# Triangular inverses of two recurrent mixers: substitution on VectorE, or doubling on TensorE

## The chip, the cores and the metric

One core of a Trainium2 chip runs the whole program in one launch. The metric is the device time of that core in microseconds (us). Engines are named as in the profile: PE (TensorE) multiplies, PEld is its weight load, DVE is VectorE, ACT is ScalarE, POOL is GpSimd, SP is SyncE, whose queue issues nearly all DMAs.

## The reference

One layer of a decoder runs over 1024 prompt tokens and 8 sequences of 4 sample tokens:

```python
h = rms_norm(x) * (1 + scale_m) + shift_m
p_a, p_b, p_c = split(h @ w_in)
y_a = rwkv7(p_a)           # mixer A: 6 heads x 64, delta rule
y_b = gated_deltanet(p_b)  # mixer B: 6 heads x 64, delta rule
y_c = hgrn2(p_c)           # mixer C: 4 heads x 64, gated, no delta rule
x = x + gate_m * (concat(y_a, y_b, y_c) @ w_out)
x = x + gate_f * ((silu(h2 @ w_gate) * (h2 @ w_up)) @ w_ffn_out)
```

The delta rule makes each token's update depend on the tokens before it. Computed by chunks of 64 tokens, a head and a chunk need the inverse of a 64x64 lower triangular matrix with ones on its diagonal (`triangular_solve` with `IA = A + eye` in the reference of mixer B; mixer A's loop over tokens is brought to the same form). With 17 chunks (16 of the prompt, one that holds the sample tokens) and 6 + 6 heads that is 204 inverses.

## The kernel before, in words

Arrays lie with channels or tokens on the 128 partitions; two heads are handled at a time, one on partitions 0 to 63 and one on 64 to 127. So mixers A and B are three pairs of heads each, C is two pairs. A pair is cut into three segments of 6, 6 and 5 chunks. A segment goes through three stages, which are the parts of `seg_a`, `seg_b`, `seg_c` between their `yield`s: stage 0 prepares whole-segment arrays, stage 1 finishes the inverses, stage 2 runs the recurrence chunk by chunk. The main loop writes stage 2 of one segment, stage 1 of the next and stage 0 of the one after beside each other, together with the projections `p` of the next pair (`dense`), which are wide PE products of 128x128 weights with 384, 288 or 296 columns, float32 as three passes over rounded halves. Behind the mixers come the output projection and the feed-forward part, in two halves of the columns (`ffn_input`, `ffn_up`, `down`), where nearly all is wide PE products with 264 columns; their weights are split into halves `wh` and `wl` by ACT, and by DVE or POOL.

The inverses, in `invert` (line 769), called by `seg_a` and `seg_b` for one segment of two heads: the four diagonal 32x32 blocks of every chunk are written to DRAM (`mb`, 4 DMAs) and read back so that each partition holds a block and every fourth column of it (`int`, 4 DMAs); a DMA sets the start of the result `ix`. DVE then substitutes through 31 columns with two instructions each (into `itq`, then into `ix`), under `nc.priority(SUBHI)`, which sets them ahead of other DVE work. The result goes back through DRAM (`tb`, 4 + 4 DMAs), DVE transposes a part (`its`), and the lower left 32x32 blocks are found by two rounds of 32x32 products on PE with ACT copies behind them.

No order is written by hand. The class `Plan` records all operations with their tiles; `Plan.order` simulates the five engines with the prices of `Plan.cost` and picks at each step the recorded operation that comes first and is ready; `emit` writes them down, and each engine then works through its list in order. Tiles of a tag are given out in the order of recording: `psm`, `psd`, `psg`, `psc` (lines 676 to 686) are two PSUM banks each, all eight there are. `mm2` (line 721) is one 64x64 product for each of the two heads, one behind the other; a float32 product is two matmuls in the trace. All operations carry line 626, that of `emit`, so rows are told apart by tiles.

Of the kernel before, what the change touches and what calls it, by code (L numbers as in the profile page):

```python
# [21 lines left out]
P = 128  # L22
# [21 lines left out]
NG = 4  # L44
FG = 2
NINT = 1
SUBHI = 3000
NITQ = 1
NITS = 2
NIX = 2  # L50
# [56 lines left out]
for _nm, _w in (("ident", 128), ("ones", 128), ("ind", 16),  # L107
                ("m3", 192), ("m3s", 192), ("neg", 64), ("negs", 64),
                ("sel1", 8), ("sel2", 8), ("reset", 448), ("bones", 128), ("bmean", 128), ("xinit", 512)):
    MASK_COLS[_nm] = (_n, _w)  # L110
    _n += _w
# [4 lines left out]
def mask_arrays():  # L116
# [31 lines left out]
    xi = np.zeros((P, 2, 8, 32))  # L148
    for v, nb in enumerate((24, 20)):
        for cg in range(NG):  # L150
            for j in range(8):
                xi[nb * cg:nb * cg + nb, v, j, NG * j + cg] = 1.0
    put("xinit", xi.reshape(P, 512))
# [26 lines left out]
class Tile:  # L180
    def __init__(self, plan, tag, dt):
        self.plan, self.tag, self.dt = plan, tag, dt
        self.slot = self.fresh = self.ap = None
        self.first = None          # first op
        self.left = 0
        self.ops = []
        self.end = 0
        self.writes, self.reads = [], []


class View:
    """a view of a tile whose place is not decided yet; kept as the view of the first place and the way to it"""
# [37 lines left out]
class Op:  # L230
    __slots__ = ("i", "eng", "fn", "args", "kw", "pre", "succ", "npre", "hold", "lat", "ready", "prio", "cols", "wait", "dense", "new", "tiles",
                 "label", "end", "start", "after", "x", "next", "load")
# [10 lines left out]
class Plan:  # L243
    """stands for nc and the tile pools while a program is written down"""
# [27 lines left out]
    def give(self, tag, to, cut):  # L272
        """once the last tile of tag is done with, the parts that cut makes of its places hold tiles of the tag to"""
# [14 lines left out]
    # ---- what a view covers  # L288
    def cover(self, v):
# [12 lines left out]
        if m is None:  # L302
            m = 1
            for s, n in dims:
# [13 lines left out]
    # ---- writing down  # L318
# [29 lines left out]
    def glue(self, ops):  # L348
        """to be issued one right after the other, once all of them can be"""
# [14 lines left out]
    def dep(self, o, p, kind):  # L364
        # kind 2: result needed, 1: only the order matters
# [32 lines left out]
    # ---- prices  # L398
    def cost(self, o):
# [7 lines left out]
        e = o.eng  # L407
        if e == "tensor":
# [11 lines left out]
            # hold: how long the next one has to wait; load: how long after the one before the weights are there  # L420
# [45 lines left out]
    # ---- the order  # L466
    def order(self):
# [12 lines left out]
        # queue of the tiles of each tag  # L480
# [16 lines left out]
        bw = [0.0]  # L497
        warm = {}
# [34 lines left out]
        while len(seq) < n:  # L533
# [109 lines left out]
class Step:  # L643
# [7 lines left out]
    # tiles of one tag are given out in program order, so every stream of work has its own  # L651
# [27 lines left out]
    def psm(self):  # L679
        return self.nc.tile("ps", [P, 512], F32, "psm", 2)  # L680
# [8 lines left out]
    def load_consts(self, par, masks, lora):  # L689
# [6 lines left out]
        self.masks = masks  # L696
# [28 lines left out]
    def tokens(self, arrs, c, nch):  # L725
        """chunk c of each array [(h, d), tokens] -> psum [64 tokens, array, h, d]; two chunks are turned at once"""
# [8 lines left out]
    def headsum(self, x, n, which="bones", alloc=None):  # L735
        """sum or mean over the channels of a head, on each of its channels; the ones are exact in float32r"""
# [8 lines left out]
    def sigmoid(self, out, x, nbias=0.0, sign=1.0):  # L745
        """sigmoid(sign * x - nbias) from the one table set that has exp and ln"""
# [12 lines left out]
    def table(self, name, behind=None, before=None):  # L759
        """load a set of functions, behind one activation and before another"""  # L760
# [7 lines left out]
    # tt[(h,s), c, t] holds N^T, N = -(strictly lower part); on return it holds ((I - N)^-1)^T  # L768
    def invert(self, tt, nc_):
        nc = self.nc  # L770
        nb = 4 * nc_
        mb = self.nc.tile("dr", [2, 2, nc_, 32, 32], F32, f"mb{nc_}", 3)
        for h in (0, 1):
            for b in (0, 1):
                o = CH * h + 32 * b
                nc.sync.dma_start(mb[h, b].rearrange("c s t -> s c t"), tt[o:o + 32, :, 32 * b:32 * b + 32])
        nt = self.nc.tile("sb", [P, 32, 32], F32, "int", NINT)
        mf = mb.rearrange("h b c s t -> (h b c) s t")
        for cg in range(NG):
            nc.sync.dma_start(nt[nb * cg:nb * cg + nb], mf)  # L780
        # one 32x32 block and every fourth column of it per partition:
# [1393 lines left out]
```

## Time and profile before

| | us |
|---|---|
| median of 3 runs | 1865.06 |
| lowest and highest of them | 1862.27, 1881.21 |
| profiled execution, first to last instruction | 1864.7 |
| PE busy in it | 1715.9 (92%) |
| DVE busy | 1557.1 (84%) |
| ACT busy | 952.0 (51%) |
| POOL busy | 958.8 (51%) |

The profile gives no other time of its execution than that span. A busy share is a mean over stages with different limits; up to about 100 us the inputs come in, from there to about 920 us the mixers run, behind them the output projection, and from 1065 us on the feed-forward part. Matmul ends are modelled, so PE counts as busy for longer than a matmul keeps the next one waiting.

### The profile page before, as it was taken

The page shows a single profiled execution, that of the slowest core. Times are in us where ns is not written, and L with a number is a line of the kernel's source. Part 1 is how long each engine was busy: PE and PEld are TensorE (multiplying, and loading weights), DVE is VectorE, ACT ScalarE, POOL GpSimd, SP SyncE. Part 2 cuts the span into 40 slices and gives each one's busy share as a digit, 9 for nine tenths or more (in the row PEclk, how much of TensorE's full clock was granted, in tenths as well). Part 3 has the DMA queues.
Part 4 walks back from the last instruction along what each step waited for, and adds up shares of the span by engine and source line. Part 5 has one row for each costly group of instructions (what it writes and reads, how often), then busy time and mean ns, then how long its engine had stood idle before and what let it go on. Part 6 is the DMA issues. An engine that isn't in the chain of part 4 may idle for free.

```text
span 1864.7 us, 42417 instructions
## 1 busy us (share of the span) xinstructions
PE 1715.9 (92%) x15462; PEld 1483.8 (80%) x15462; DVE 1557.1 (84%) x3981; ACT 952.0 (51%) x2383; POOL 958.8 (51%) x1089
## 2 busy tenths in 40 slices
PE   4999999899899789899999999999998889999996
PEld 2777766667677677677679999999998789999995
DVE  6776688879879877887776999889999999899998
ACT  4543454655556455656874655444444543443444
POOL 5542333433335544636523866656567555555555
PEclk8989999889999898999989999999999799999998
DMA  7424123123224222211353222323232132232231
GB/s 264 124 64 116 39 62 109 49 68 113 59 77 127 55 63 55 57 34 39 102 155 115 66 93 95 108 91 109 91 103 69 62 115 79 91 108 85 87 108 65
DMA packets 151242, 166.56 MB, mean 89 GB/s; under 512 B 65941, under 2 KB 91161, under 8 KB 151033
## 3 DMA queue, kind: packets, MB, share of 16 engines
q1 hardware_dynamic: 150456, 163.27, 28.8%
q8 instruction: 121, 1.98, 0.5%
q14 instruction: 89, 0.72, 0.1%
q10 hardware_dynamic: 576, 0.59, 0.1%
HBM read 149.23 MB, written 14.57 MB: 88 GB/s over the span
## 4 chain that ended last, share of the span: by engine, by line
PE 52%; DVE 28%; issue 6%; POOL 5%; ACT 4%; SPq 2%; DMA 2%; DVEq 0%; POOLq 0%; ACTq 0%
PE psd L626 16%; PE psc L626 13%; PE psm L626 11%; PE psg L626 11%; DVE sl L626 6%; DVE itq L626 5%; DVE ix L626 5%; DVE kp L626 3%; SPq L626 2%; POOL wl L626 2%; DVE s L626 2%; ACT sl L626 2%; DVE wl L626 2%; DVE wr L626 2%; DVE act L626 1%
## 5 line engine op out<-in xcount | busy, mean ns | idle before, releaser
L626 PE MATMUL psd<-act,wh 128*128 128x384 f32 (+3 forms) x2144 | 552.8, 334 | 13.2 <-ACT act L626 7.4
L626 PEld LDWEIGHTS psd<-act,wh 128*128 128x128 f32 x2144 | 373.9, 195 | 40.8 <-ACT act L626 8.9
L626 POOL TENSOR_TENSOR wl<-wr,wh 128x512 fp32r<-128x512 f32 (+1 forms) x216 | 300.7, 1396 | 192.1 <-ACT wh L626 177.3
L626 PE MATMUL psd<-act,wl 128*128 128x384 f32 (+3 forms) x1048 | 348.9, 333 | 5.3 <-DVE wl L626 3.8
L626 ACT ACTIVATE sl<-sl 128x384 f32<-128x384 f32 (+5 forms) x400 | 188.1, 484 | 129.2 <-DVE sl L626 101.4
L626 ACT CAST wh<-wr 128x512 fp32r<-128x512 f32 (+1 forms) x280 | 170.7, 615 | 109.0 <-PE psd L626 27.8
L626 PEld LDWEIGHTS psd<-act,wl 128*128 128x128 f32 x1048 | 203.7, 194 | 21.2 <-DVE wl L626 6.2
L626 DVE TENSOR_TENSOR itq<-int,ix 96x66 f32<-96x66 f32 (+26 forms) x558 | 170.7, 306 | 27.1 <-DMA int<-mb 15.9
L626 DVE TENSOR_TENSOR ix<-ix,itq 96x66 f32<-96x66 f32 (+26 forms) x558 | 164.7, 295 | 9.6
L626 PE MATMUL psg<-act,wh 128*128 128x264 f32 (+2 forms) x784 | 154.2, 290 | 5.3 <-DVE act L626 4.0
L626 PE MATMUL psc<-act,wh 128*128 128x264 f32 (+2 forms) x776 | 152.4, 289 | 0.8 <-DVE act L626 0.6
L626 PE MATMUL psm<-act,wh 128*128 128x264 f32 (+1 forms) x760 | 147.8, 288 | 2.7 <-ACT act L626 1.3
L626 POOL TENSOR_TENSOR sl<-sl,sl 128x384 fp32r<-128x384 f32 (+5 forms) x84 | 85.5, 1019 | 101.2 <-ACT sl L626 39.2
L626 PEld LDWEIGHTS psg<-act,wh 128*128 128x128 f32 x784 | 124.6, 191 | 7.5 <-DVE act L626 4.9
L626 ACT CAST raw<-sl 128x264 fp32r<-128x264 f32 x88 | 36.3, 413 | 173.7 <-DVE sl L626 92.5
L626 PEld LDWEIGHTS psc<-act,wh 128*128 128x128 f32 x776 | 123.1, 190 | 2.4 <-DVE act L626 1.1
L626 PEld LDWEIGHTS psm<-act,wh 128*128 128x128 f32 x760 | 119.5, 190 | 4.5 <-ACT act L626 1.5
L626 POOL TENSOR_TENSOR wl<-int,wh 128x512 fp32r<-128x512 f32 (+1 forms) x63 | 87.9, 1398 | 61.1 <-ACT wh L626 61.0
L626 PE MATMUL psc<-act,wl 128*128 128x264 f32 (+2 forms) x388 | 113.4, 292 | 5.4 <-DVE wl L626 3.7
L626 PE MATMUL psg<-act,wl 128*128 128x264 f32 (+2 forms) x392 | 114.0, 291 | 2.6 <-DVE wl L626 2.1
L626 PE MATMUL psm<-act,wl 128*128 128x264 f32 (+1 forms) x380 | 110.2, 290 | 4.4 <-DVE wl L626 3.0
L626 ACT COPY ts<-psg 64x128 f32<-64x128 f32 (+1 forms) x272 | 75.9, 279 | 69.1 <-PE psc L626 46.1
(324 smaller groups left out, 4481.3 us busy)
## 6 DMA issues: line engine op xcount, KB each, us to landing
wr<-in_w_fi_dram SPq DMA_DIRECT2D x87, 256.0 KB
wr<-in_w_ada_dram SPq DMA_DIRECT2D x80, 256.0 KB
wr<-in_w_in_dram SPq DMA_DIRECT2D x62, 256.0 KB
wr<-in_w_fo_dram SPq DMA_DIRECT2D x51, 256.0 KB
int<-in_w_fi_dram SPq DMA_DIRECT2D x46, 256.0 KB
kp<-in_xT_dram SPq DMA_DIRECT2D x32, 192.0 KB
tq<-in_w_fi_dram SPq DMA_DIRECT2D x23, 256.0 KB
s<-in_w_fi_dram SPq DMA_DIRECT2D x20, 256.0 KB
```

The source lines that it names most:

```text
L626: getattr(getattr(nc, o.eng), o.fn)(*[real(a) for a in o.args], **{k: real(a) for k, a in o.kw.items()})
```

## The change

`invert` is written anew. It starts from the identity and doubles the size of the inverted diagonal blocks: for blocks of 1 it copies the places one below the diagonal; for blocks of 2, 4, 8, 16 and 32 it forms `T N T` on PE, with a DVE transpose in front and an ACT copy between, and writes the places that the level's mask names (`lvm`, in use by mixer C before) with `copy_predicated` on DVE. It is recorded as a whole in stage 1. `N` is masked as it leaves PSUM. The DRAM round trips, `itq`, `its` and the initial values are gone; `int` has two tiles (`NINT`), `ix` one. Of the two `psm` banks one becomes `psi`, which the inverses use for both products of a level; mixer C takes `psi` and `psm` in turn, and the feed-forward part goes through banks in a cycle of eight.

The planner's prices change too: a wide matmul holds PE for its columns plus 12 ns (3 before), each 64x64 product 58 ns (110 and 27 before), and operations of POOL that read SBUF and operations of DVE that read two SBUF operands (or one, for copies and `tensor_scalar`) get a `port`, which only one of them at a time can hold in the simulated order. Comments and docstrings are removed as well; the other constants that set engines in the feed-forward part stay.

```diff
-NINT = 1
-SUBHI = 3000
+NINT = 2
+NIX = 1
...
+        o.port = e == "gpsimd" and len(sb) > 0 or e == "vector" and (
+            len(sb) > 1 or len(sb) == 1 and o.fn in ("tensor_scalar", "tensor_copy"))
...
-                o.hold = max(M, n) / 2.4 + 3 if n >= 256 else max(M / 1.2, n / .6)
+                o.hold = max(M, n) / 2.4 + 12 if n >= 256 else max(M / 1.2, n / .6)
...
-                o.hold = 27 if p0 >= 64 else 2 * max(M, n) / 1.2 + 3
+                o.hold = 2 * max(M, n) / 2.4 + 5
...
+            if o.port:
+                tm = max(tm, port)
+                port = tm + o.hold
...
     def psm(self):
-        return self.nc.tile("ps", [P, 512], F32, "psm", 2)
+        return self.nc.tile("ps", [P, 512], F32, "psm", 1)
+
+    def psi(self):
+        return self.nc.tile("ps", [P, 512], F32, "psi", 1)
...
+    def inverse_tiles(self, n):
+        x = fl(self.nc.tile("sb", [P, 6, P], F32, "int", NINT))
+        return x[:, 0:n], x[:, 384:384 + n]
+
+    def invert(self, tt, nt, t, nch):
+        nc = self.nc
+        n = nch * CH
+        c3 = lambda a: a.rearrange("p (c t) -> p c t", t=CH)
+        fill = lambda li, x: nc.vector.copy_predicated(
+            c3(tt), self.lvm[:, 0, li].unsqueeze(1).broadcast_to([P, nch, CH]), c3(x))
+        nc.scalar.copy(c3(tt), self.lvm[:, 0, 6].unsqueeze(1).broadcast_to([P, nch, CH]))
+        fill(0, nt)
+        for li in range(1, 6):
+            nc.vector.transpose(t, tt)
+            px = self.psi()
+            for c in range(nch):
+                sl = slice(c * CH, (c + 1) * CH)
+                self.mm2(px[:, sl], nt[:, sl], t[:, sl], True, True)
+            x = self.nc.tile("sb", [P, 384], F32, "ix", NIX)[:, 0:n]
+            nc.scalar.copy(x, px[:, 0:n])
+            py = self.psi()
+            for c in range(nch):
+                sl = slice(c * CH, (c + 1) * CH)
+                self.mm2(py[:, sl], x[:, sl], tt[:, sl], True, True)
+            fill(li, py[:, 0:n])
...
-        nc.vector.tensor_copy(tt, pm[:, 0:n])
+        nt, ti = self.inverse_tiles(n)
+        cp = nch - (si == 2)
+        nc.vector.tensor_tensor(t3(nt)[:, 0:cp], t3(pm[:, 0:n])[:, 0:cp],
+                                self.m("m3")[:, 0:CH].unsqueeze(1).broadcast_to([P, cp, CH]), op=ALU.mult)
...
-        next(inv, None)
+        self.invert(tt, nt, ti, nch)
...
-            pa = self.psm()
+            pa = (self.psm, self.psi)[li % 2]()
...
-        return (self.psd, self.psg, self.psc, self.psm)[self.turn % 4]()
+        return (self.psd, self.psg, self.psc, self.psm, self.psd, self.psg, self.psc, self.psi)[self.turn % 8]()
```

DVE's list in the middle of the mixers, before: the substitution of one segment stands between the other work of two stages.

```order
L626 TENSOR_TENSOR ix_169<-ix_169,itq_170 96x5x12
L626 TENSOR_TENSOR gs_180<-psg_152,msk_63 128x192
L626 TENSOR_TENSOR itq_170<-int_113,ix_169 96x6x11
L626 SCALAR_TENSOR_TENSOR sl_312_11426<-raw_229_8027,par_90,sl_312_11426 128x256
L626 TENSOR_TENSOR ix_169<-ix_169,itq_170 96x6x11
L626 TENSOR_TENSOR kp_79<-psm_111,sl_298_10956 128x384
L626 TENSOR_TENSOR itq_170<-int_113,ix_169 96x6x10
L626 SCALAR_TENSOR_TENSOR sl_291_10835<-sl_291_10835,sl_308_11124 128x384
L626 TENSOR_TENSOR ix_169<-ix_169,itq_170 96x6x10
L626 TENSOR_TENSOR kp_65<-sl_291_10835,gb_154 128x384
```

DVE's list now, at an inverse of a mixer A segment (`kp_69` is its `tt`, `S` the recurrence's state, `sd` the decayed one):

```order
L624 TENSOR_SCALAR sd_180<-S_168,dl_163 128x64
L624 COPY_PREDICATED kp_69<-lvm_93,psi_165 128x320
L624 SCALAR_TENSOR_TENSOR sl_191_7110<-sl_189_7054,par_90,raw_139_4654 128x384
L624 STREAM_TRANSPOSE int_113<-kp_69 128x320
L624 TENSOR_REDUCE mod_89<-psm_111 128x9 x2
L624 TENSOR_SCALAR mod_89<-mod_89,par_90 128x9 x2
L624 SCALAR_TENSOR_TENSOR S_167<-psc_117,dl_163,sd_180 128x64
L624 TENSOR_SCALAR sd_181<-S_167,dl_163 128x64
L624 COPY_PREDICATED kp_69<-lvm_93,psi_165 128x320
L624 STREAM_TRANSPOSE int_113<-kp_69 128x320
L624 SCALAR_TENSOR_TENSOR S_169<-psc_118,dl_163,sd_181 128x64
```

The 62 instructions of a substitution have given way to six predicated copies and five transposes, and other segments' work stands between them.

PE's list before, around the products of one inverse (`psd<-act,wh` and `psd<-act,wl` are projections):

```order
L626 MATMUL psc_118<-its_174,kp_73 32x32
L626 MATMUL psd_151<-act_123,wh_101 128x296
L626 MATMUL psd_151<-act_124,wh_101 128x296
L626 MATMUL psm_111<-msk_63,sl_114_2960 128x128 x2
L626 MATMUL psc_118<-its_174,kp_73 32x32 x11
L626 MATMUL psd_151<-act_123,wl_105 128x296
L626 MATMUL psd_151<-act_125,wh_101 128x296
L626 MATMUL psd_151<-act_126,wh_101 128x296
L626 MATMUL psd_151<-act_125,wl_105 128x296
L626 MATMUL psd_151<-act_127,wh_103 128x296
L626 MATMUL psc_117<-kp_73,its_174 32x32
L626 MATMUL psd_151<-act_128,wh_103 128x296
```

PE's list now, around one level of an inverse:

```order
L624 MATMUL psd_151<-act_121,wh_101 128x384
L624 MATMUL psi_165<-int_112 64x64 x12
L624 MATMUL psd_151<-act_122,wh_101 128x384
L624 MATMUL psd_151<-act_121,wl_105 128x384
L624 MATMUL psd_151<-act_123,wh_101 128x384
L624 MATMUL psd_151<-act_124,wh_101 128x384
L624 MATMUL psm_111<-wr_96,ct_88 32x256 x2
L624 MATMUL psm_111<-wr_98,ct_88 32x256 x2
L624 MATMUL psd_151<-act_123,wl_105 128x384
L624 MATMUL psi_165<-kp_66,ix_166 64x64 x12
L624 MATMUL psd_151<-act_125,wh_101 128x384
```

In place of two rounds of 32x32 products in a segment there are ten sets of 64x64 products, each for six chunks of two heads, with projections and other narrow work between them.

## Rows read from the trace of the kernel before

**Rows 1.** The page: its first line.
```profile
span 1864.7 us, 42417 instructions
```

**Rows 2.** Busy time by stretch: us, each engine's us (instructions), PEclk granted, DMA share.
```profile
100.00:860.00 760.00, 695.07 (x7152) 531.04 (x7153) 608.79 (x1942) 403.72 (x1150) 319.37 (x504) 0.94 0.26 71
860.00:920.00 60.00, 58.98 (x738) 43.38 (x736) 38.89 (x93) 46.54 (x140) 35.64 (x60) 1.00 0.22 67
920.00:1065.00 145.00, 141.09 (x1265) 125.68 (x1265) 107.82 (x235) 83.79 (x226) 72.99 (x89) 0.95 0.40 120
1065.00:1400.00 335.00, 331.42 (x2680) 327.49 (x2679) 304.89 (x593) 162.23 (x334) 204.46 (x148) 1.00 0.30 96
1520.00:1850.00 330.00, 314.69 (x2509) 307.70 (x2508) 303.93 (x723) 142.57 (x284) 189.51 (x139) 1.00 0.27 87
```

**Rows 3.** Chain of waits, 600 to 700 us: share of the stretch by line.
```profile
by line: PE psd L626 16.3%; DVE ix L626 14.4%; DVE itq L626 12.8%; DVE sl L626 8.2%; SPq L626 7.7%; PE psc L626 7.5%; DMA int<-mb 5.6%; issue 4.4%; POOL sl L626 2.9%; ACT sl L626 2.5%; POOL wl L626 2.1%; POOL sd L626 2.0%; PE psm L626 2.0%;
```

**Rows 4.** Timeline of DVE: start us, us, engine, line, operation, out<-in.
```profile
604.93 0.93 DVE L626 TENSOR_TENSOR itq<-int,ix 80x42 f32<-80x42 f32 x1
605.89 0.93 DVE L626 TENSOR_TENSOR ix<-ix,itq 80x42 f32<-80x42 f32 x1
...
611.47 0.18 DVE L626 TENSOR_TENSOR ix<-ix,itq 80x24 f32<-80x24 f32 x1
```

**Rows 5.** Timeline of POOL at the same time.
```profile
605.76 1.00 POOL L626 TENSOR_TENSOR kp<-sl,sl 128x384 f32<-128x384 f32 x1
```

**Rows 6.** Timeline of PE, with the idle time before in brackets.
```profile
612.13 0.34 PE L626 MATMUL psd<-act,wh 128*128 128x384 f32 x1
615.22 1.01 PE L626 MATMUL psm<-sl,kp 64*64 64x64 f32 x14 [2.74 <-DVE sl L626]
```

**Rows 7.** Busy time just behind that wait.
```profile
615.00:618.00 3.00, 2.79 (x28) 2.67 (x29) 2.58 (x4) 0.33 (x1) 2.63 (x6) 0.50 0.35 83
```

**Rows 8.** Groups by line: xcount | busy us, mean ns | idle before.
```profile
L626 DVE TENSOR_TENSOR itq<-int,ix 96x66 f32<-96x66 f32 (+26 forms) x558 | 170.7, 306 | 27.1 <-DMA int<-mb 15.9 <-DMA kp<-tb 1.8
...
L626 DVE TENSOR_TENSOR ix<-ix,itq 96x66 f32<-96x66 f32 (+26 forms) x558 | 164.7, 295 | 9.6
...
L626 DVE STREAM_TRANSPOSE its<-kp 32x192 f32<-32x192 f32 (+1 forms) x36 | 12.7, 354 | 3.6 <-DMA kp<-tb 3.0
...
L626 DVE COPY_PREDICATED kp<-lvm,psm 128x384 f32<-128x384 uint8 (+5 forms) x48 | 23.4, 499 | 7.8 <-PE psm L626 7.6
...
L626 ACT COPY raw<-psd 128x384 f32<-128x384 f32 (+4 forms) x110 | 40.5, 389 | 36.6 <-PE psd L626 35.6
...
L626 PEld LDWEIGHTS psc<-kp,its 32*32 32x32 f32 x408 | 10.6, 111 | 6.6 <-issue 2.1 <-ACT sl L626 1.8 <-ACT its L626 1.0
```

**Rows 9.** Timeline of PE: a set of 24 narrow matmuls between wide ones.
```profile
683.63 0.34 PE L626 MATMUL psd<-act,wl 128*128 128x384 f32 x1
683.80 0.33 PE L626 MATMUL psd<-act,wh 128*128 128x384 f32 x1
684.06 0.91 PE L626 MATMUL psm<-sl,kp 64*64 64x64 f32 x24
684.91 0.45 PE L626 MATMUL psd<-act,wh 128*128 128x384 f32 x1
```

**Rows 10.** Timeline of PE: narrow pairs one behind the other.
```profile
563.29 0.28 PE L626 MATMUL psc<-kp,S 64*64 64x64 f32 x4
563.40 0.28 PE L626 MATMUL psm<-sl,kp 64*64 64x64 f32 x4
```

**Rows 11.** Chain of waits over the span: start us, us, what.
```profile
1191.26 1.79 DVE wr L626
...
1223.83 1.80 DVE int L626
...
1592.48 1.76 DVE wr L626
...
1626.90 1.76 DVE s L626
```

More of the change, by code (lines that the diff above doesn't have):

```diff
@@ L147, in mask_arrays @@
     put("reset", np.broadcast_to(r, (P, 448)))
[L148 to L153, printed above, removed]
     lv = np.zeros((P, 2, 7, CH), np.float32)
@@ L231 @@
     __slots__ = ("i", "eng", "fn", "args", "kw", "pre", "succ", "npre", "hold", "lat", "ready", "prio", "cols", "wait", "dense", "new", "tiles",
-                 "label", "end", "start", "after", "x", "next", "load")
+                 "label", "end", "start", "after", "x", "next", "load", "port")
 class Engine:
@@ L407, in cost @@
         e = o.eng
+        sb = [a for a in list(o.args[1:]) + list(o.kw.values()) if isinstance(a, View) and self.space[a.t.tag] == "sb" and size(a) > 1]
+        o.port = e == "gpsimd" and len(sb) > 0 or e == "vector" and (
+            len(sb) > 1 or len(sb) == 1 and o.fn in ("tensor_scalar", "tensor_copy"))
         if e == "tensor":
@@ L497, in order @@
         bw = [0.0]
+        port = 0
         warm = {}
@@ L765, in table @@
             self.nc.after(p, before)
-    def invert(self, tt, nc_):
+    def inverse_tiles(self, n):
+        x = fl(self.nc.tile("sb", [P, 6, P], F32, "int", NINT))
+        return x[:, 0:n], x[:, 384:384 + n]
+    def invert(self, tt, nt, t, nch):
         nc = self.nc
[L771 to L780, printed above, removed]
-        x = self.nc.tile("sb", [P, 8, 32], F32, "ix", NIX)
-        tq = self.nc.tile("sb", [P, 8, 32], F32, "itq", NITQ)
-        np_ = nb * NG
-        o = MASK_COLS["xinit"][0] + (0 if nc_ == 6 else 256)
-        nc.sync.dma_start(fl(x)[0:np_], self.masks[0:np_, o:o + 256])
-        with nc.priority(SUBHI):
-            for j in range(31):
-                ni = 31 - j
-                m = j // NG + 1
-                nv = nt[0:np_, j:j + 1, j + 1:32].broadcast_to([np_, m, ni])
-                xv = x[0:np_, 0:m, j:j + 1].broadcast_to([np_, m, ni])
-                nc.vector.tensor_tensor(tq[0:np_, 0:m, 0:ni], nv, xv, op=ALU.mult)
-                nc.vector.tensor_tensor(x[0:np_, 0:m, j + 1:32], x[0:np_, 0:m, j + 1:32], tq[0:np_, 0:m, 0:ni], op=ALU.add)
-        tb = self.nc.tile("dr", [nb, 8, NG, 32], F32, f"tb{nc_}", 3)
-        for cg in range(NG):
-            nc.sync.dma_start(tb[:, :, cg], x[nb * cg:nb * cg + nb])
-        tv = tb.rearrange("(h b c) m g i -> h b c (m g) i", h=2, b=2)
-        ts = self.nc.tile("sb", [P, 6, 32], F32, "its", NITS)
-        for h in (0, 1):
-            o = CH * h
-            for b in (0, 1):
-                nc.sync.dma_start(tt[o + 32 * b:o + 32 * b + 32, :, 32 * b:32 * b + 32],
-                                  tv[h, b].rearrange("c j i -> j c i"))
-            nc.vector.transpose(ts[o:o + 32, 0:nc_], tt[o:o + 32, :, 0:32])
-            nc.gpsimd.memset(tt[o + 32:o + 64, :, 0:32], 0.0)
-        yield
-        pa = self.psc()
-        pb = self.psc()
-        for c in range(nc_):
-            for h in (0, 1):
-                o = CH * h
-                nc.tensor.matmul(pa[o + 32:o + 64, 32 * c:32 * c + 32],
-                                 tt[o:o + 32, c, 32:64], ts[o:o + 32, c, :], start=True, stop=True)
-        for h in (0, 1):
-            o = CH * h
-            nc.scalar.copy(fl(ts[o + 32:o + 64, 0:nc_]), pa[o + 32:o + 64, 0:32 * nc_])
-        for c in range(nc_):
-            for h in (0, 1):
-                o = CH * h
-                nc.tensor.matmul(pb[o:o + 32, 32 * c:32 * c + 32],
-                                 ts[o + 32:o + 64, c, :], tt[o + 32:o + 64, c, 32:64], start=True, stop=True)
-        for h in (0, 1):
-            o = CH * h
-            nc.scalar.copy(tt[o:o + 32, :, 32:64], pb[o:o + 32, 0:32 * nc_].rearrange("p (c t) -> p c t", t=32))
@@ L1250, in seg_b @@
         yield
-        next(inv, None)
+        self.invert(tt, nt, ti, nch)
         nc.gpsimd.tensor_tensor(ttv, ttv, bt[:, c0:c1].unsqueeze(2).broadcast_to([P, nch, CH]), op=ALU.mult)
@@ L1549, in ada @@
         if early == "int":
-            e = fl(nc.tile("sb", [P, 32, 32], F32, "int", NINT))
+            e = [fl(nc.tile("sb", [P, 6, P], F32, "int", NINT))[:, 0:512] for i in (0, 1)]
         for qt in range(4):
@@ L1557, in ada @@
             else:
-                xv = e[:, 256 * (qt - 1):256 * (qt - 1) + 512] if early == "int" and qt % 2 else fl(self.wr())
+                xv = e[qt // 2] if early == "int" and qt % 2 else fl(self.wr())
                 xv = xv.rearrange("p (k n) -> p k n", n=256)
@@ L2051 @@
         nc.give(tag, "wr", lambda ap: [fl(ap)[:, o:o + KH * P].rearrange("p (k n) -> p k n", n=P)
-                                       for o in range(0, ap.shape[1] * ap.shape[2], KH * P)])
+                                       for o in range(0, ap.shape[1] * ap.shape[2] - KH * P + 1, KH * P)])
     nc.order()
```

16 lines of the change are left out of this document (4 added, 12 removed).

## The prediction

> **What bounds the kernel now.** I start from the busy time by stretch [rows 2]. Behind 1065 us PE is full: its weight load is busy 327 of 335 us, 98%, at a granted clock of 1.00. In the mixers, from 100 to 860 us, PE counts as busy for 695 of 760 us, but matmul ends are modelled; the weight load, which must run once for every matmul, is busy for 531 us, 70%. So the array is not full where the change works. It could hold more matmuls, and something else decides when they come.
>
> What that is, the chain of waits tells [rows 3]: from 600 to 700 us a quarter of it is the substitution (`ix` and `itq` 27%) and another 13% is SP's queue and the landing of `int`, most of which is the same inverse's way through DRAM. The groups by line give its size [rows 8]: 558 + 558 instructions, 170.7 + 164.7 = 335 us of DVE's 609 in this stretch.
>
> The reader should then see why these are so dear. Free of POOL such an instruction takes 0.18 us; while POOL adds and multiplies, it takes 0.93 us and ends when POOL's does [rows 4, 5]: 604.79 + 1.00 and 605.76 + 1.00 on POOL, 604.93 + 0.93 and 605.89 + 0.93 on DVE. At 0.20 us each 1116 instructions would take 223 us, so about 112 of the 335 us are waits behind POOL. Since the substitution has priority in the planned order, other DVE work comes late, and PE's list stands still: it waits 2.74 us for `sl` [rows 6], and just behind that wait the granted clock is 0.50, the 1.2 GHz level [rows 7]. Over 760 us the mean is 0.94 [rows 2], so 12% of the time, 91 us, went at the lower level, where wide products take twice as long: 46 us are lost to that.
>
> **The change part by part.** Removed from DVE: 335 us and 12.7 us of small transposes [rows 8]. Added per inverse of a segment, 18 times: six predicated copies and five transposes. The copies cost 0.50 us each [rows 8], 108 of them 54 us. A transpose of 128x384 is not in the trace: the nearest row has 32x192 at 0.354 us [rows 8], so it lies between that and twice as much, 0.71; I take 0.52, close to the copy of as many columns, 90 of them 47 us (32 to 64). DVE's 609 us become about 609 - 348 + 101 = 362, 48% of the stretch. The masking of `N` takes the place of a copy of the same size. ACT gains 108 copies of 0.389 us [rows 8], 42 us on 404 of 760: hidden by its idle time; without that they would lengthen each level by 0.4 us. It loses 72 small copies, for which I count nothing. SP loses 17 DMAs per inverse, 306 in all, counted in the code, and POOL two small memsets per inverse.
>
> PE gains 10 products per chunk and pair of heads: 102 chunks make 1020 `mm2`, 4080 matmuls. Pairs one behind the other start 0.11 to 0.12 us apart [rows 10], 117 us in all. A set of six pairs alone between wide products takes 684.06 to 684.91, 0.85 us [rows 9]; 170 such sets make 145 us. I take 125, nearer the first, for a reason that follows. The 32x32 products leave: two groups of 10.6 us of weight load [rows 8], of which one is shown. Net +104 us, bounds +96 and +124.
>
> So the load that PE has to carry in this stretch goes from 531 to 635 us. At today's 70% fill the stretch would take 907 us, 147 more; at the feed-forward part's 98% it would take 648, 112 less. **Break-even is a fill of 635/760 = 84%.** Which fill comes? For a low one speaks the stretch from 860 to 920 us, where no substitution runs and the load share is 43/60 = 72% [rows 2]; but there ACT is at 78%, and the planned order leaves only 163 of the 2208 wide projection products behind the last inverse to fill gaps with. In the new order 480 stand there. For a high one speaks the next stretch, 920 to 1065 us: 126/145 = 87%, with DVE at 74% and a mix of waits. I take that, 87%: 635/0.87 = 730, **-30 us**. DVE falls to half its load, the priority that made the rest late is gone, and half of the time at the lower clock should go with the waits before it; this lies within the 87%. For the range I keep 79% (804, +44) and 95% (668, -92).
>
> The switch between wide and narrow products has a price of its own: wide ones follow each other by 0.17 us, the first narrow one comes 0.26 us behind a wide one, and a set is 0.85 where six pairs make 0.69 [rows 9, 10]. That is 0.25 us for each stretch of narrow work among wide. The Trainium skill, "TensorEngine Tiling (Array Packing)", section Key Properties, says that a change of tiling mode drains the engine, which speaks against 180 new sets; by that rule, with every set a stretch of its own, the price is 180 x 0.25 = 45 us, and the sum below would be +2 instead of -43. The trace agrees on the drain. But counted over PE's whole list between the first and the last projection, stretches of narrow work go from 520 to 460: most sets stand beside other narrow rows. So I add nothing for it.
>
> An inverse's time: before, 62 instructions at 0.3 us [rows 8] are 19 us, and three ways through the queue besides. Now five levels, each a transpose (0.52), two sets (0.85 or less), an ACT copy (0.39) and a predicated copy (0.50), with some 0.25 us of handing over at each of five places (an estimate from the 0.26 us behind a wide matmul): 4.4 us, 22 us for an inverse. Eighteen of them, all through the one `psi` bank, make 390 of 760 us: the bank can hold that, and what is late next is the chain of chunks behind it, not the bank.
>
> The stretch of mixer C gains a little from the 317 products more that are left to fill it: 60 us x (87 - 72)% = 9 us at most, nothing at least; I take -4.
>
> In the feed-forward part only the planned order moves (port, 12 ns, cycle of banks). Its first half repeats every 32.57 us (1191.26 to 1223.83), its second at 34.42 (1592.48 to 1626.90) [rows 11] with a load share of 98% and 93% [rows 2]. The work per period is the same on PE; DVE has 16 small additions more. If the new order mended all of it, 330/34.42 = 9.6 periods x 1.85 = 18 us would go. DVE is busy for 304 of 330 us there [rows 2], part of it behind POOL, and only that part can be mended, so I take half, **-9**, bounds -18 and +9 (an order that avoids overlaps in the plan and brings weights later).
>
> Sum: -30 - 4 - 9 = -43 on the span of 1864.7 us [rows 1]. The median of the runs is 1865.06, 0.4 above it, so the forecast is 1822 us.
>
> **The rivals.**
> No change: PE fills to 81 to 84%. The stretch then takes 756 to 784 us, and with -13 elsewhere the time is 1848 to 1876, middle 1862. For it: PE counted as busy 91% already, and 104 us come on top. Against it: the 70%.
>
> Slower, by the single banks. Before, `psm` had two: while one was read, the next product went into the other. Now about 137 products of the mixers (5 per segment of A, 4 of B, 4 of C, 2 for each of 16 modulation jobs) take turns in one, and 180 sets in `psi`. After each PE must find other work for as long as the reader takes, 0.50 us [rows 8], and a handover of 0.25: 317 x 0.75 = 238 us, and tiles are given out in the order of recording, so that a late one holds up all behind it. It decides as soon as more than 30/238 = 13% of that is exposed; with a third, 79 us, the time is 1822 + 79 = 1901. For it: the 72% between 860 and 920, and 2208 products that must be spread over all gaps. Against it: DVE, the reader of many, has half its load. The Trainium skill, "Perfetto Trace Analysis", section Matmuls, asks to rotate independent groups through different banks so that reading one overlaps the next group; by that rule alone two serial products on one bank are the wrong choice. No run so far shows one bank.
>
> The change doesn't do what it says: the planned port is no lock on the chip, so DVE and POOL meet as before. Then the feed-forward part gives 0 instead of -9, 1831. I give that 4 in 10 within each case; it moves none to another side by itself.
>
> **How the numbers follow.** Runs of this kernel can be told apart at about 1%: 1846 and 1884. Forecast 0.57 (its own range 1765 to 1846), no change 0.20, slower 0.23. The range reaches from a 95% fill, 1864.7 - 92 - 9 = 1764, to the slower rival, 1905; faster 0.57, same 0.20, slower 0.23.
>
> **What would show it.** Right: no `itq`; DVE near half of the mixer stretch; sets of 24 matmuls on `psi` within 0.9 us; the weight load at 84% or more there and granted clock above 0.95; no PE wait for `sl` above 2 us; the second feed-forward half below 34 us a period. Wrong: PE waiting for ACT or DVE in front of `psm` and `psi` products for more than 30 us in sum, a load share that stays near 75%, or a transpose above 0.71 us.

## Result and the profile after

The changed kernel takes **1873.57 us** (median of 20 runs, 1870.91 to 1876.53). Beside it the kernel before took 1857.26 (20 runs, 1851.52 to 1881.21): the ratio is **1.0081, 95% interval 1.0071 to 1.0092**, slower by 16 us. The forecast was 1822. The profiled run of before (1865.06) lies 7.8 us above its median, so the two traces differ by 5.9 us of span only. Its granted clock over the span was 0.953; runs of before that took about 1858 us had 0.956 to 0.959, so I put these 7.8 us down to more time at the low clock than usual, as an estimate. The traces still show where 43 us of forecast gain went.

First line of the page, answering to [rows 1], and the busy time by stretch, in the columns of [rows 2]:

```profile
span 1870.6 us, 47447 instructions
```

```profile
100.00:860.00 760.00, 756.33 (x10649) 598.93 (x10647) 462.81 (x1033) 436.64 (x1244) 301.30 (x480) 1.00 0.19 57
860.00:920.00 60.00, 60.00 (x494) 53.09 (x493) 30.73 (x55) 36.37 (x88) 26.51 (x36) 1.00 0.26 77
920.00:1065.00 145.00, 135.94 (x1351) 125.04 (x1350) 106.29 (x241) 85.49 (x227) 74.31 (x99) 0.98 0.34 103
1065.00:1400.00 335.00, 330.57 (x2638) 323.83 (x2638) 302.41 (x585) 157.97 (x324) 207.14 (x148) 1.00 0.31 96
1520.00:1850.00 330.00, 319.28 (x2508) 310.50 (x2507) 295.52 (x713) 142.71 (x283) 189.66 (x138) 0.99 0.29 87
```

In the mixers every sign of a stalled PE is gone: busy 756 of 760 us (695 before), granted clock 1.00 (0.94). DVE fell from 609 to 463 us. And yet the weight load is busy for 79% only. The mixers' last narrow product starts at 974.0 us before and at 974.6 after, so one window holds the mixers of both; first before, then after:

```profile
100.00:974.00 874.00, 806.00 (x8440) 612.59 (x8440) 688.61 (x2129) 488.10 (x1408) 372.95 (x592) 0.94 0.27 75
```

```profile
100.00:974.00 874.00, 862.45 (x11767) 688.69 (x11765) 537.23 (x1193) 513.02 (x1453) 351.84 (x558) 1.00 0.21 62
```

The same stretch of time holds 3327 more matmuls; DVE's 151 us less are worth nothing. The chain of waits from 600 to 700 us answers to [rows 3]: it is PE from end to end.

```profile
by line: PE psd L624 48.4%; PE psi L624 24.6%; PE psc L624 12.8%; PE psm L624 8.7%; PE psg L624 5.8%
```

What waits is now the other side. All waits of PE from 100 to 935 us, and two rows of all engines' waits (us in total, times, longest):

```profile
PE psm L624 <- DVE kp L624: 1.7, 3, 0.7
PE psd L624 <- ACT sl L624: 1.6, 1, 1.6
PE psi L624 <- DVE kp L624: 1.5, 1, 1.5
PE psm L624 <- ACT sl L624: 1.2, 1, 1.2
PE psm L624 <- DMA wr<-in_w_ada_dram: 0.3, 1, 0.3
PE psm L624 <- ACT tk L624: 0.2, 1, 0.2
...
DVE kp L624 <- PE psi L624: 55.7, 49, 3.2
ACT ix L624 <- PE psi L624: 53.7, 43, 4.9
```

PE waits 6.5 us in all; the inverses wait for PE. Groups by line from 100 to 935 us, answering to [rows 8]:

```profile
L624 PE MATMUL psi<-int 64*64 64x64 f32 x2040 | 88.1, 222 | 0.0
L624 PE MATMUL psi<-kp,ix 64*64 64x64 f32 x2040 | 84.2, 222 | 0.0
...
L624 DVE COPY_PREDICATED kp<-lvm,psi 128x384 f32<-128x384 uint8 (+2 forms) x103 | 57.7, 561 | 65.7 <-PE psi L624 55.7 <-ACT sl L624 4.4 <-ACT us L624 1.6
L624 DVE STREAM_TRANSPOSE int<-kp 128x384 f32<-128x384 f32 (+1 forms) x90 | 49.2, 548 | 0.6
```

The parts cost what was forecast: 4080 matmuls, transposes 49 us (47 forecast), predicated copies 0.56 us (0.50). So do the sets, in PE's timeline:

```profile
640.46 0.68 PE L624 MATMUL psm<-sl,kp 64*64 64x64 f32 x16
640.98 0.87 PE L624 MATMUL psi<-int 64*64 64x64 f32 x24
641.68 0.40 PE L624 MATMUL psm<-sl,kp 64*64 64x64 f32 x8
...
642.64 0.33 PE L624 MATMUL psd<-act,wh 128*128 128x384 f32 x1
642.90 0.92 PE L624 MATMUL psi<-kp,ix 64*64 64x64 f32 x24
643.75 0.44 PE L624 MATMUL psd<-act,wh 128*128 128x384 f32 x1
```

A set among narrow products takes 0.70 us (640.98 to 641.68). Between wide ones it takes 0.85, and the wide one ahead of it holds PE for 0.26 instead of 0.17.

**PE's time taken apart.** For every trace I split the time between 100 us and the mixers' last narrow product, from each matmul's start to the next one's. *Work* is what the shape takes among its equals (0.17 us for 128x384, 29 ns for a 64x64 record, 10.5 for one of 32x32 in quarters, 16 in the kernel before). The excess over it is a *change of shape* if the next matmul has another array shape (at most 0.2 us each), a *wait* above 0.2 us, *low clock* where the granted clock is 0.50, and *rest*. Pauses and changes of shape in a stretch at the low clock stand in that column alone, and the numbers in brackets leave those changes out (with them there are 1048 before and 1039 in the changed kernel). From 100 to 974 us of the changed kernel the profile has PE idle for 11.6 us (874.00 - 862.45); in the rest of the 21 us of waits PE counts as busy, since ends are modelled. In us:

| kernel | runs (median) | mixers end | work | changes (number) | waits | low clock | rest |
|---|---|---|---|---|---|---|---|
| before | 1857 | 974.0 | 570 | 122 (959) | 77 | 63 | 42 |
| changed | 1874 | 974.6 | 682 | 126 (1035) | 21 | 4 | 41 |
| sets_twice | 1995 | 1091.1 | 803 | 121 (1006) | 22 | 4 | 42 |
| turn_twice | 1886 | 985.9 | 683 | 128 (1058) | 25 | 7 | 44 |
| inv32 | 1861 | 960.6 | 640 | 152 (1262) | 23 | 10 | 35 |
| mixed6 | 1885 | 975.7 | 639 | 123 (988) | 48 | 22 | 43 |
| mixed6_lock | 1882 | 982.1 | 643 | 104 (875) | 54 | 37 | 44 |
| mixed6_lock_runs10 | 1879 | 985.2 | 647 | 75 (646) | 68 | 58 | 37 |
| before_newplan | 1942 | 1048.8 | 575 | 96 (785) | 106 | 133 | 39 |
| after_noport | 1912 | 1002.2 | 679 | 128 (1042) | 37 | 14 | 44 |
| after_oldplan | 1952 | 1060.0 | 679 | 141 (1117) | 53 | 38 | 49 |
| two_banks | 1965 | 1059.6 | 679 | 123 (1022) | 55 | 54 | 50 |
| setglue | 1860 | 965.6 | 685 | 114 (959) | 17 | 11 | 40 |
| runs6 | 1835 | 937.8 | 685 | 93 (833) | 16 | 5 | 39 |
| long_runs | 1849 | 949.9 | 684 | 76 (660) | 43 | 14 | 33 |
| glue_runs10 | 1859 | 961.7 | 685 | 76 (660) | 31 | 37 | 32 |
| glue_runs16 | 1899 | 997.7 | 688 | 74 (602) | 74 | 29 | 33 |
| blocks_runs16 | 1911 | 1017.3 | 646 | 96 (775) | 78 | 73 | 26 |
| before_runs6 | 1887 | 995.1 | 567 | 85 (704) | 109 | 94 | 41 |
| blocks_runs6 | 1818 | 919.0 | 641 | 117 (1054) | 14 | 13 | 35 |

The first two lines are the result: 112 us of work came, 56 us of waits and 59 us of low clock went, and the 122 us of changes stayed.

### The profile page after: what moved, and what is told of

Read it like the earlier page. It is cut to its first block, busy times and chain, and to the rows that moved or that the text cites. A ratio compares the mean times of both kernels' runs of the same rounds, so it can differ in the third digit from the quotient of the medians.

```text
span 1870.6 us, 47447 instructions
## 1 busy us (share of the span) xinstructions
PE 1782.7 (95%) x18726; PEld 1562.3 (84%) x18726; DVE 1385.9 (74%) x3030; ACT 979.4 (52%) x2423; POOL 935.4 (50%) x1050
## 4 chain that ended last, share of the span: by engine, by line
PE 80%; DVE 10%; ACT 4%; issue 2%; DMA 2%; POOL 1%; SPq 0%; DVEq 0%; ACTq 0%; POOLq 0%
PE psd L624 29%; PE psc L624 15%; PE psg L624 13%; PE psi L624 12%; PE psm L624 10%; DVE sl L624 3%; DVE kp L624 3%; DVE wl L624 1%; ACT wh L624 1%; ACT sl L624 1%; DVE act L624 1%; DMA wr<-in_w_ada_dram 1%; DVE raw L624 1%; ACT L624 1%; DVE s L624 1%
## 5 line engine op out<-in xcount | busy, mean ns | idle before, releaser
L624 POOL TENSOR_TENSOR wl<-wr,wh 128x512 fp32r<-128x512 f32 (+1 forms) x203 | 283.8, 1403 | 242.5 <-ACT wh L624 227.1
L624 ACT ACTIVATE sl<-sl 128x384 f32<-128x384 f32 (+4 forms) x400 | 186.9, 483 | 52.7 <-DVE sl L624 45.3
L624 POOL TENSOR_TENSOR wl<-int,wh 128x512 fp32r<-128x512 f32 (+1 forms) x75 | 104.9, 1401 | 92.9 <-ACT wh L624 85.1
L624 POOL TENSOR_TENSOR sl<-sl,sl 128x384 fp32r<-128x384 f32 (+6 forms) x84 | 83.7, 996 | 127.9 <-DVE sl L624 65.4
L624 ACT CAST wh<-int 128x512 fp32r<-128x512 f32 x112 | 68.6, 616 | 80.5 <-PE psg L624 26.7
L624 DVE COPY_PREDICATED kp<-lvm,psi 128x384 f32<-128x384 uint8 (+2 forms) x110 | 61.0, 555 | 65.7 <-PE psi L624 55.7
L624 DVE TENSOR_TENSOR sl<-sl,sl 128x264 f32<-128x264 f32 (+2 forms) x136 | 97.0, 721 | 13.4 <-ACT sl L624 12.4
L624 PE MATMUL psi<-int 64*64 64x64 f32 x2040 | 88.1, 222 | 0.0
L624 PEld LDWEIGHTS psi<-int 64*64 64x64 f32 x2040 | 71.6, 134 | 19.8 <-issue 10.8
L624 PEld LDWEIGHTS psi<-kp,ix 64*64 64x64 f32 x2040 | 69.7, 135 | 18.4 <-issue 9.2
```

The source lines that it names most:

```text
L624: getattr(getattr(nc, o.eng), o.fn)(*[real(a) for a in o.args], **{k: real(a) for k, a in o.kw.items()})
```

## Experiments

Theory A: PE is full, a microsecond of its work or of its changes of shape is a microsecond of the end. Rivals: the chain of one inverse through its single bank (B), or something else while PE has room (C). A ratio is to the kernel before, timed beside each run, with its 95% interval. The median of the kernel before was 1857 to 1860 us in every set of runs, so differences to the changed kernel's 1873.57 hold to about 3 us.

### More work on PE, more work on DVE

```diff
+                for _ in (0, 1):                     # sets_twice, for px and for py
                     self.mm2(px[:, sl], nt[:, sl], t[:, sl], True, True)
...
             nc.vector.transpose(t, tt)
+            nc.vector.transpose(t, tt)               # turn_twice
```

> The changed kernel with each product of the inverses issued twice into the same place: 170 sets of 24 matmul records more on PE, each 0.70 us long by the changed kernel's timeline (640.98 to 641.68), and nothing more for any other engine. Theory A (PE is full in the mixers: waits below 7 us there, granted clock 1.00): the whole 170 x 0.70 = 119 us come out at the end, 1985 to 2000. Theory B (the chain of one inverse through the single psi bank decides): 10 sets x 0.70 = 7 us more on an inverse of some 40 us, with other work beside it; 18 in a row give up to 126, so that A and B agree here unless PE has room, and the run with doubled transposes tells them apart. Theory C (PE still has room, something else decides): below 40 us.

> The changed kernel with each of the 90 transposes of the inverses done twice on DVE: 0.55 us more at each level of an inverse and 49 us more DVE work, nothing more on PE. Theory A (PE is full): within 10 us of the changed kernel's 1873.6, since DVE is at 61% in the mixers. Theory B (the chain of the inverses decides): 18 inverses in a row, each 2.7 us longer, give 49 us, 1915 to 1925.

`sets_twice` took 1994.9 us, 121 more than the changed kernel, as A has it to 2 us. `turn_twice` took 1886.1, 12.5 more: 2.5 over A's bound (4 us of waits, 3 of low clock and 2 of changes of shape more), far from B's 49. The chain through `psi` is not the limit; PE is.

### Less work on PE: 32x32 blocks

```diff
-                self.mm2(px[:, sl], nt[:, sl], t[:, sl], True, True)
+                self.mm4([(px[o:o + 32, 32 * c:32 * c + 32], v[o:o + 32, c, o % CH:o % CH + 32],
+                           tv[o:o + 32, c, o % CH:o % CH + 32]) for o in (0, 32, 64, 96)])
```

> The changed kernel with the same ten products per inverse cut to 32x32 blocks: for the first four levels the four diagonal blocks of a chunk as four matmuls on four quarters of the array, for the last one the 32x32 corner product. Transposes, predicated copies and their number stay. A set of 24 records of 32x32 took 0.40 us in the kernel before, one of 64x64 0.70. If four of them run side by side, 170 sets get 0.30 us shorter: theory A gives 51 us less than 1873.6, about 1822, and the weight-load share says nothing of it. If they go two by two, a set of the first levels takes 0.8 us and theory A gives 1870 to 1885. Theory C (something other than PE decides): 1870 to 1876 whatever a set takes.

1860.5 us (ratio 1.0016, 0.9998 to 1.0035), 13 less than the changed kernel; none of the three expectations. PE's timeline of this kernel shows a set of 48 records, 0.55 us to the next start; the four quarters run side by side in part.

```profile
639.74 0.34 PE L624 MATMUL psd<-act,wh 128*128 128x384 f32 x1
640.01 0.62 PE L624 MATMUL psi<-kp,ix 32*32 32x32 f32 x48
640.56 0.33 PE L624 MATMUL psc<-sd,ts 64*64 64x64 f32 x4
```

Work fell by 42 us, and a third shape brought 227 changes more, 26 us. The difference, 16, is near the 13 seen. That made the changes of shape the next question.

### Fewer changes of shape

One number of the planner: once a wide product is taken, at least so many follow where there are any. `setglue` binds the twelve products of a set in the order; `glue_runs16` and `glue_runs10` do both; the blocks are `inv32`.

```diff
-        run, RUN = 0, int(self.params.get("run", 0))
+        run, RUN = 0, int(self.params.get("run", 6))      # runs6; 10 in long_runs; 16
...
-                self.mm2(px[:, sl], nt[:, sl], t[:, sl], True, True)
+            self.mset([(px[:, sl], nt[:, sl], t[:, sl]) for sl in cs])   # setglue: one glued list
```

> The changed kernel with one number of the planner set: once a wide product is chosen, at least ten wide ones follow where there are any. The work is the same; the planned PE list changes between wide and narrow shapes 689 times instead of 1046. In the changed kernel's trace a narrow product that is followed by a wide one, and a wide one followed by a narrow one, each start the next about 0.1 us later than between equals (642.64 to 642.90 and 642.90 to 643.75 beside 0.17 and 0.70). Theory A (PE is full, and the changes of shape are part of what fills it): 357 x 0.1 = 36 us less than 1873.6, 1830 to 1845. The theory of the prediction (the changes of shape can be left out of the sum): within 8 us of 1873.6. A rival: narrow work comes later, the chain of chunks decides instead, 1880 or more, with waits before psc and psm products.

> The changed kernel with the twelve matmuls of a set bound together in the planned order. In the changed kernel's trace the 180 sets lie in 278 pieces; the planned list has 970 changes of shape instead of 1046. Theory A: 76 x 0.1 = 8 us less than 1873.6, 1860 to 1870. If changes of shape cost nothing: within 4 us.

> The changed kernel with the sets bound together and at least sixteen wide products in a row: 642 changes of shape in the planned list, against 1046 of the changed kernel (1873.6), 689 with runs of ten (1848.7) and 970 with bound sets (1859.9). Theory A: 404 x 0.1 = 40 us less at most, 1833 to 1846. If runs that long make the chain of chunks late: waits before psc, psi or psg products above 40 us and 1850 or more.

> The same with the products cut to 32x32 blocks, whose sets took 0.55 us from start to the next product instead of 0.70 to 0.85 but brought a third shape (1278 changes; now 883, 163 fewer than the changed kernel). Theory A: 42 us less for the products and 17 us less for the changes, 1873.6 - 59 = 1815 at best, 1815 to 1840. If the third shape eats it: like the run without blocks, 1833 to 1846.

> The changed kernel with runs of at least six wide products where there are any: 859 changes of shape in the planned list, against 1046 (1873.6) and 689 with runs of ten (1848.7). If changes of shape are the floor: 187 x 0.1 = 19 us less, 1852 to 1860, between the two. If the gain of the runs of ten came from another order by chance: anything outside 1848 to 1874.

> The changed kernel with bound sets and runs of ten: 722 changes of shape. If the loss of the run with sixteen came from the length of the runs: like long_runs, 1840 to 1855. If it came from binding the sets beside long runs (a bound set can start only when all its operands are there, and a run holds it off): 1865 to 1900 with more than 50 us of waits.

`long_runs` 1848.7 (ratio 0.9939, 0.9918 to 0.9960) and `setglue` 1859.9 (1.0009, 0.9995 to 1.0023): 25 and 14 us less than the changed kernel; A's numbers were 4 us lower for the one and just above for the other. `glue_runs16` 1898.9 (1.0210) and `blocks_runs16` 1911.2 (1.0275) went the other way, to none of A's ranges: few changes (602 and 775), but waits of 74 and 78 us and more low clock. `runs6` gave **1834.8 (0.9873, 0.9843 to 0.9902)**, better than I expected (1852 to 1860): 33 us less in changes, 5 less in waits, and the mixers end 37 us sooner. It lies in the range (outside 1848 to 1874) that I had set aside for a gain by another order by chance. Against chance speaks that the changes saved account for 33 of the 37 us; the other lengths, below, show that the order counts as well. Against the changed kernel's row above, its weight load in the same window rose from 689 to 719 us, but that window now holds 36 us of the output projection too:

```profile
100.00:974.00 874.00, 865.08 (x12076) 719.32 (x12075) 548.03 (x1231) 525.34 (x1476) 366.48 (x570) 1.00 0.23 68
```

`glue_runs10` came to 1858.6 (0.9999): as many changes as `long_runs`, and between my two cases. So runs of ten and more are paid twice: PE waits longer (31 to 78 us against 16 with six), as if narrow work that others wait for came late, and more of its time is at the low clock (14 to 73 us against 5). Six is the best length tried; the lengths between were not.

### Part of the work back on DVE

The middle segment of every mixer A and B (six of eighteen inverses) goes by substitution again.

```diff
+ROWS = lambda m, g, si: si == 1
...
-        self.invert(tt, nt, ti, nch)
+        if ROWS("a", g, si):
+            next(inv, None)                 # the substitution of the kernel before
+        else:
+            self.invert(tt, nt, ti, nch)
```

> The changed kernel with the middle segment of each mixer A and B (36 of 102 chunks, 6 of 18 inverses) solved by substitution on DVE again, as in the kernel before, and the planner without the lock for the port (with it the substitution cost the kernel before 84 us). Theory A (PE is full in the mixers, DVE has room at 61%): 36/102 x 119 = 42 us less PE work and some 110 us more on DVE, 1825 to 1845. The rival: six substitutions bring back the waits and the lower clock of the kernel before, in which case 1850 to 1875.

> Six of eighteen inverses by substitution on DVE, and the planner with the lock as in the changed kernel; 920 changes of shape in the planned list. Theory A (PE full, a microsecond of work is worth a microsecond): 43 us less work (639.4 against 682.5 in the mixers of the run without the lock) and 126 x 0.1 = 13 us less for changes of shape, 1820 to 1850. The rival: under the lock each of 372 substitution instructions waits in the plan for POOL, as in the kernel before under the new planner (84 us for 1116): 28 us back, 1850 to 1880, or more with waits before psc.

> The same with runs of at least ten wide products; 728 changes of shape. Theory A: 19 us less than the run without the runs, and 25 us less if the gain of the runs of ten adds up in full. If waits decide once PE has room: no gain over mixed6_lock, or a loss.

1885.0 (1.0140), 1881.7 (1.0128) and 1878.8 (1.0113): A's forecast is wrong in all three. The rival's mechanism is right, though `mixed6` lies 10 us above its range and `mixed6_lock` 2 us. 35 to 43 us of work are off PE, and waits and low clock take them: 70, 91 and 126 us against 25 in the changed kernel. The window of `mixed6_lock`, to be read beside the changed kernel's:

```profile
100.00:974.00 874.00, 829.20 (x10556) 659.28 (x10554) 553.24 (x1500) 504.07 (x1434) 370.03 (x569) 0.97 0.23 66
```

PE busy falls to 829 us and the clock to 0.97. A microsecond of PE work was worth a microsecond only where nothing late stood behind it. All three were compared under planners that were not tuned to them.

### The planner's half, the lock and the banks

```diff
-            if o.port:                      # after_noport; after_oldplan: old prices too
-                tm = max(tm, port)
-                port = tm + o.hold
...
-        return self.nc.tile("ps", [P, 512], F32, "psm", 1)    # two_banks
+        return self.nc.tile("ps", [P, 512], F32, "psm", 2)
...
-        return self.nc.tile("ps", [P, 512], F32, "psi", 1)
+        return self.psm()
```

> The kernel before with only the planner's new prices and its lock for the port that DVE and POOL share; the substitution stays. Theory A (the whole loss lies in the inverses' PE work, the planned order gives nothing): within 8 us of the kernel before, 1850 to 1865. The prediction's step for the feed-forward part: 9 us less than the kernel before. If the new order itself costs time (the last products of the feed-forward part end 9 us later in the changed kernel's trace): 8 to 16 us more.

> The changed kernel without the planner's lock for the port that DVE and POOL share; prices and inverses stay. The prediction gave the order with the lock 9 us in the feed-forward part, so that without it the kernel would come out 9 us later, 1878 to 1888. Theory A (the lock moves DVE work that PE does not wait for): within 6 us of 1873.6. The kernel before lost 84 us by prices and lock together; if the lock alone does that with the new inverses too, the kernel without it is 20 us or more faster.

> The changed kernel's inverses with the planner of the kernel before: old prices, no lock. With the kernel before, the kernel before under the new planner (1942) and the changed kernel (1873.6) it closes a square of four. If the two halves of the change simply add up: 1857 + (1873.6 - 1942) = 1789. Theory A (the inverses' products fill PE, whatever the order): 1860 to 1915; its planned list changes shape 1178 times instead of 1046, 132 x 0.1 = 13 us more than the changed kernel at least, so I expect the upper half.

> The changed kernel with one tag of two banks in turn for all products that go to psm and psi now (the inverses, the small products of the mixers, the feed-forward part's cycle). The slower rival of the prediction (a single bank makes PE wait for its reader, 79 us and more): 30 us or more below 1873.6. Theory A (PE waits below 7 us in the mixers, none for a bank): within 8 us; its planned list changes shape 44 times more, 4 us.

None of these four runs fell into any of the cases that I had written down; sums of work did not tell what an order costs. `before_newplan`, the kernel before with the new prices and the lock, took 1942.1 (1.0444, 1.0419 to 1.0470): 84 us more. `after_oldplan` took 1951.9 (1.0489), 78 more than the changed kernel. So the square has 1858, 1942, 1952 and 1874 in its corners: each half alone costs 84 to 94 us, and the two together 16. The doubling alone costs 94 us under the old planner and gains 68 under the new one. Work is the same for one inverse under both planners (570 and 575, 682 and 679 us); what moves most is waits and low clock, 140 to 239 us for the substitution and 25 to 91 for the doubling. `after_noport`, 1911.9 (1.0286), gives the lock alone 38 us with the new inverses: 28 in the mixers, 10 behind them. Why the lock helps one inverse and harms the other I did not take apart.

`two_banks` took 1965.1 (1.0552), 92 us more. I had expected the same time, and the prediction's slower rival a gain. So a bank of its own for the inverses is an advantage here. The run shows waits 34 us and low clock 50 us higher, and 85 of the 92 us in the mixers. The likely reason is that in one tag places are given in the order of recording, so that a set that is late holds up every small product behind it; this is read from the planner's rule, not shown by another run. The Trainium skill, "Perfetto Trace Analysis", section Matmuls, asks to rotate groups through different banks; here the measurement speaks against a rotation that puts the inverses and the other small products into one queue.

### The two that close it

> The kernel before (substitution, old planner) with runs of at least six wide products; its planned list changes shape 815 times instead of 1052. In its mixers PE lost 77 us in longer pauses and 62 us to the low clock beside 122 us in changes of shape. Theory A (there PE is not full, the substitution's lateness decides): the changes saved turn into waits, within 15 us of 1858 or slower. If the floor by changes of shape holds it as well: 24 us less, 1828 to 1840.

> The changed kernel with runs of six (1834.8) and the products cut to 32x32 blocks: 42 us less product work (640 against 682 in the mixers), 1090 changes of shape in the planned list instead of 859. Theory A: 231 x 0.1 = 23 us back, 19 us less in the sum, 1810 to 1830. If the order or waits eat it: 1830 to 1860.

`before_runs6` took 1887.1 (1.0146, 1.0119 to 1.0172), 28 us more than the kernel before: 37 us less in changes, 32 more in waits, 31 more at the low clock. Its largest waits of PE, 100 to 935 us:

```profile
PE psc L626 <- DVE S L626: 21.7, 25, 2.4
PE psg L626 <- DVE s L626: 19.0, 13, 2.8
PE psg L626 <- DVE gs L626: 10.5, 8, 3.7
```

With the substitution PE was not full, and what is saved on it turns into waiting, in these rows for DVE. With the doubling it is full, and the same number gains 39 us. `blocks_runs6` took **1817.9 us, ratio 0.9786 (0.9765 to 0.9806)**: 44 us less work than `runs6`, 221 changes and 24 us of them more, 17 us less in the end. This is theory A's range. It beats both kernels: 42 us below the kernel before, 56 below the changed one.

## Why the prediction was wrong

**The step that failed is "Which fill comes?".** I read 30% of idle weight load as room and let it fill to 87%, a share borrowed from 920 to 1065 us. It came to 79% with PE never idle: 599 of 760 us. Of PE's 874 us in the mixers before, 570 were work; of the other 304, 164 were changes of shape and rest, which no further work can use, and 140 waits and low clock, which it can. 115 of these 140 were won, and 112 of work and 4 of changes put in their place: nothing was left of the -30.

The borrowed stretch was no measure for a mix. The mixers run on to 974.0 us, not to about 920 as I wrote ahead of the prediction, so it joins the mixers' tail to the output projection, here in the columns of [rows 2]:

```profile
920.00:974.00 54.00, 51.96 (x553) 38.18 (x552) 40.94 (x96) 37.84 (x120) 17.95 (x30) 0.87 0.51 149
974.00:1065.00 91.00, 89.13 (x716) 87.50 (x713) 66.89 (x140) 45.95 (x107) 55.05 (x59) 1.00 0.33 103
```

That is 71% in the tail and 96% where all products are wide; the 87% held for neither. The load to be carried was no fixed sum either: before, the weight load of a wide projection takes 188 ns at the full clock and 330 at the low one (medians), so it shrinks when the clock is cured. From 100 to 974 us it came to 689 us, not to 612.6 + 104 = 717. PE's own busy time, 695 of 760 at 0.94, was much nearer: 65 us idle and 46 us lost to the clock are 111, against a net +104. I named that under "No change" and gave it 0.20, because modelled ends made me distrust it.

**The changes of shape.** "So I add nothing for it" was right as a difference: 1048 before and 1039 after, or 959 and 1035 at the full clock, 4 us. What I missed is that those already there were no room: 122 us for 959 changes, 0.13 each, and `runs6` shows that they are on the path. The Trainium skill, "TensorEngine Tiling (Array Packing)", section Key Properties, says that a change of tiling mode drains the engine. The later starts fit that; that it is a drain no row shows.

**The terms beside it.** PE's added work, +104 (96 to 124), measures 112 net. DVE's 362 came out as 463: the 80 groups that both kernels have in equal number from 100 to 974 us became longer, 368 to 397 us in sum, and the rest of the 101 us I did not take apart; PE waits little for DVE (3.2 of the 6.5 us above). The load share of at least 84% is refuted, DVE near half of the stretch (61%) and the period below 34 us (34.1, the mean time for 264 products in the second half) are missed. The clock above 0.95, whole sets within 0.9 (72 of 73), transposes below 0.71 and no wait for `sl` above 2 us are confirmed: the signs of a cured stall, without the gain.

**The feed-forward part**, forecast at -9, went the other way. By the starts of the 6592 products with 264 columns (8 to 50%, 50 to 62, 62 to 96, and from there to the end of the span), the changed kernel needs +4.5, +1.9, -1.7 and +5.0 us, +9.7 in sum; the first 8% come 3.8 us sooner. The lock does what I gave it, 10 us in the second half, as its absence shows (300.5 against 290.5 us). But it only gives back what the new prices take there: `after_oldplan`, with neither, needs 291.0, and the kernel before 292.2. The first half gets longer with the new plan also in `before_newplan` (346.1, 350.6 and 350.4). The 5 us at the very end were not followed up.

**The rivals.** "No change" was the mechanism that came, at 1862 in the middle and 1848 to 1876 at its ends. The median lies inside, with a fill below its 81%; as a difference, +16 us to the median of before lies above its upper end of +11. The single banks were wrong: PE waits 6.5 us in all. "The planned port is no lock" was wrong too: without it the kernel is 38 us slower, though its 0 for the feed-forward part was nearer than my -9.

## What to carry to other kernels

An idle share is not room until it is split: for the bounding engine add up the work by shape, the changes of shape, the waits and the low clock, and set new work against the last two alone. A share from another stretch holds only where the mix of shapes is the same. A stall cured by more work on the engine that stalled gives back at most the stall. When that engine is full at full clock, the next thing to change is the order: here one number (runs of six) gave 2% on the changed kernel and cost 1.5% on the one before.

## What was not expected of the hardware

Four 32x32 products on four quarters of the array take at most 0.09 us a chunk (0.55 for six, the change of shape included), where a pair of 64x64 ones takes 0.117 (0.70 for six). The low clock goes with waiting as a second price: in the table its column holds 4 to 13 us where waits were below 26 us, and 29 to 133 us in the eight kernels with waits of 54 us or more. Part of it is pauses that fall into such stretches, most in `before_newplan`.
